# Letting the filter steps of a convolution lead TensorE a little in the source's order, in the last quarter of a two-layer encoder

## The chip, the cores and the metric

The kernel runs on one core of a Trainium2 chip. The metric is the time of one execution on the device in microseconds (us). TensorE (PE in the profile) multiplies matrices, VectorE (DVE) and ScalarE (ACT) work on rows of elements, GpSimd (POOL) adds and multiplies tiles, and SyncE (SP) issues the transfers between memory and the core.

## The reference

Two layers work on 2048 positions of 1024 channels. A layer normalizes its input, projects it to 28 groups of 128 channels, feeds four groups of heads, and projects their gated outputs back; a final normalization follows.

```python
def hybrid_layer(x, norm_g, w_in, w_out, ...):
    h = rmsnorm(x, norm_g)
    proj = jnp.einsum("bsd,de->bse", h, w_in)
    ...
    y_a = conformer_conv(a_u, a_v, ...) * jax.nn.silu(a_z)          # A: depthwise conv of width 31
    y_b = short_gated_conv(b_b, b_c, b_x, conv_b_w) * jax.nn.silu(b_z)   # B: width 3
    y_c = window_gqa(...) * jax.nn.silu(c_z)                        # C: attention in a window of 128
    y_d = neighborhood_attn(...) * jax.nn.silu(d_z)                 # D: attention on a 2-D grid
    y = jnp.concatenate([y_a, y_b, y_c, y_d], axis=-1)
    return x + jnp.einsum("bse,ed->bsd", y, w_out)

def conformer_conv(u, v, conv_w, conv_b, ln_g, ln_b):
    h = u * jax.nn.sigmoid(v)
    h = depthwise_conv(h, conv_w) + conv_b      # 31 taps
    h = layernorm(h, ln_g, ln_b)                # over the 256 channels of A
    return jax.nn.silu(h)
```

## The kernel before

Positions are cut into four chunks of 512 (0 to 3). Channels lie on partitions. Every float32 product is made of three matmuls on two rounded parts of each operand (`s0h`, `s0l` or `s1h`, `s1l` for the activations, `whi`, `wlo` for the weights), so one 128-channel tile of output for one chunk, called a job here, takes 24 matmuls `mm` of 128x512.

The work stands in eight blocks of jobs: layer 0's input projection for chunks 0 and 1 and then for 2 and 3, layer 0's output for chunks 0 and 1, and so on. The last three blocks are those of this case: layer 1's input projection for chunks 2 and 3 (28 weight tiles for two chunks, 56 jobs, "the input block"), layer 1's output for chunks 0 and 1 (16 jobs, "the first output block") and for chunks 2 and 3 (16 jobs, "the last output block").

Between the matmuls runs everything else, as Python generators that `point()` advances once per 8 matmuls:

- Attention units (`unit`, 64 in a layer): one unit treats 128 queries of two heads: scores `s`, softmax on VectorE and ScalarE, four to eight transposes `pt`, the weighted sum `o`, then `ou`, `oy` and `ag` on VectorE; after every fourth unit `ag` is stored to `Y`. Units start in a fixed order (D and C of chunk 0, D and C of chunk 1, and so on), and in the last stage every second point may start one.
- Filter steps ("taps", `tap_steps`): convolution A of a chunk and a half of its channels is 31 passes of VectorE over `accA`. `point()` emits taps while VectorE's counted time `clk["dve"]` lies behind TensorE's counted time `clk["pe"]` plus `LEAD`, which is 0. Both counters are sums of costs written into the program: every VectorE instruction adds to the one, every matmul to the other.
- Norms (`ln_steps`, `conv_ln`): when both halves of a chunk have their 31 taps, the LayerNorm of A follows: a sum on GpSimd (`lns`), a matmul with ones (`lnm`), squares, a second sum, `lnv` on TensorE, thirteen small VectorE steps for the root, `rb` on TensorE, then scale, tanh and gate (`ga` is loaded from `G`), and `accA` is stored to `Y`. Chunk 3 has a second, 15 columns wide norm for the last positions.
- A chunk's output jobs need its `Y` loaded and split (`place_y_steps`, into `s0l` or `s1l`). Chunk c's `Y` of convolution A is complete only when chunk c+1's norm is done too, since a chunk's filter is stored 15 positions late.

A scheduler then moves the instructions of each engine about, by priorities that follow the source's order, and within buffers that are handed out in the source's order: five temporaries `t`, two PSUM tiles for `s`, `lnm`, `lnv`, `rb` and `cs` together, four `accA`. So a step that stands late in the source can get its buffers only after those before it.

The first job of every odd chunk in layer 1's output waits in the source until no taps are left (`idle_until(lambda: not taps)` in `out_jobs`): it advances points and adds 1.8 to `clk["pe"]` each time.

Of the kernel before, what the change touches and what calls it, by code (L numbers as in the profile page):

```python
# [58 lines left out]
RU, RD = 3, 3  # L59
PF, UNITS, SPACING = 7, 4, 5  # L60
PF_LATE, UNITS_LATE, SPACING_LATE = 3, 6, 2
LEAD = 0.0
KSB, VTB, WB = 3, 3, 3

E_A_U, E_A_V, E_A_Z = 0, 2, 4
# [6 lines left out]
def trunk(ctx, tc, xT, w_in, w_out, par, sink, rpb, fg, trig, cmask, dmask, out):  # L72
    nc = tc.nc
    pe, act, dve, pool, sp = nc.tensor, nc.scalar, nc.vector, nc.gpsimd, nc.sync
# [37 lines left out]
    clk = {"pe": 0.0, "dve": 0.0}  # L112
# [19 lines left out]
    dve = Counted(dve)  # L132
# [37 lines left out]
    evs, bg, units, taps = [], [], [], deque()  # L170
    waiting, done = [], set()
    current, gap, points, begun, turn = [None], [0], [0], [0], [0, 0]
    pace = {"spacing": SPACING, "units": UNITS, "pf": PF}

    def advance(lst):
        for g in list(lst):
            if next(g, "end") == "end":
                lst.remove(g)

    def point():  # L180
        advance(evs)
        advance(units)
        gap[0] += 1
        points[0] += 1
        if waiting and gap[0] >= pace["spacing"] and len(units) < pace["units"] and begun[0] < turn[0] + QSB:
            group = current[0] or next((w for w in waiting if w[0]()), None)
            if group:
                current[0] = group
                gap[0] = 0
                g = group[1].popleft()()  # L190
                if not group[1]:
                    waiting.remove(group)
                    current[0] = None
                units.append(g)
                next(g)
        advance(bg)
        while taps and clk["dve"] < clk["pe"] + LEAD:
            tap()

    def tap():  # L200
        if next(taps[0], "end") == "end":
            taps.popleft()

    def idle_until(cond):
        n = 0
        while not cond():
            point()
            clk["pe"] += 1.8
            n += 1
            assert n < 4000, "nothing more happens"  # L210
# [648 lines left out]
    def run(j):  # L859
# [18 lines left out]
        for i, (k_, pt, hf, wi, k, rhs) in enumerate(seq):  # L878
            mm(pt, jb["ws"][hf][wi][:, k, :], rhs, n[k_] == 0, n[k_] == 3 * KT - 1, 0.228)
            n[k_] += 1  # L880
            if i % GRP == GRP - 1:
                g = i // GRP
                point()
                if g in work:
                    work[g]()
                for k2, p2 in zip(jb["keys"], pts):
                    if n.get(k2) == 3 * KT:
                        n[k2] = -1
                        evs.append(jb["ev"](k2[-1], p2))
# [6 lines left out]
    def in_jobs(l, half):  # L896
# [31 lines left out]
        def mark(i):  # L928
            ks = marks[i] if isinstance(marks[i], list) else [marks[i]]

            def late():
                yield from hold(8)
                for k in ks:
                    done.add(k)
            bg.append(late())
# [93 lines left out]
    then(o10[1], y_place(1, 3, 1))  # L1029

    def late():
        pace.update(spacing=SPACING_LATE, units=UNITS_LATE, pf=PF_LATE)
        return
        yield

    then(i10[1], late)

    for l in range(DEPTH):
# [138 lines left out]
```

## Time and profile before

| what | us |
|---|---|
| three runs | 2089.10, 2096.69, 2099.12 |
| median | 2096.69 |
| the profiled execution | 2092.12 |
| its span in the trace | 2090.3 |
| TensorE matmuls busy | 1967.2 (94%) |
| TensorE weight loads busy | 1638.5 (78%) |
| VectorE busy | 1553.1 (74%) |
| ScalarE busy | 1040.1 (50%) |

The profiled execution's own time is 1.8 us longer than its span. In the trace, times count from the start of the span; a line such as L135 is that of a helper through which all matmuls go, so instructions are told apart by the names of their tiles. Instructions of one group may overlap at their ends, so a sum of durations can exceed the busy time.

### The profile page before, as it was taken

How to read it: one execution, taken by the hardware profiler on the slowest of the kernel's cores; microseconds unless marked ns; L12 is line 12 of the kernel's file. 1: busy time of each engine (PE TensorE's matmuls, PEld its weight loads, DVE VectorE, ACT ScalarE, POOL GpSimd, SP SyncE). 2: the span in 40 equal slices, each digit the busy share in tenths (PEclk: the TensorE clock that was granted, in tenths of full speed). 3: DMA queues.
4: the chain of work that ended last, by engine and by line, in shares of the span. 5: the costliest groups of instructions: out<-in, count | busy, mean ns of one | idle time of the engine just before them, and what ended most of it. 6: DMA issues, size and time to landing. Idle time of an engine off the chain costs nothing.

```text
span 2090.3 us, 29475 instructions
## 1 busy us (share of the span) xinstructions
PE 1967.2 (94%) x9436; PEld 1638.5 (78%) x9436; DVE 1553.1 (74%) x3531; ACT 1040.1 (50%) x2217; POOL 181.6 (9%) x158
## 2 busy tenths in 40 slices
PE   5899999999999999899999999989999899996697
PEld 4778888787888878788888888878888788885585
DVE  6734799968985677776659998755995567866855
ACT  4435434523355466566654446532237566665542
POOL 0610000071010000000100000001000000100100
PEclk9999999999999999999999999999999999998698
DMA  9985533576455479867653467863638866577353
GB/s 281 305 280 175 150 121 92 170 257 200 151 172 171 158 246 305 242 201 236 183 164 119 143 179 220 244 197 105 179 132 252 227 193 207 154 221 221 120 177 115
DMA packets 233850, 400.65 MB, mean 192 GB/s; under 512 B 26848, under 2 KB 92000, under 8 KB 233440
## 3 DMA queue, kind: packets, MB, share of 16 engines
q1 hardware_dynamic: 233696, 398.77, 62.2%
q8 instruction: 75, 1.23, 0.3%
q14 instruction: 79, 0.65, 0.1%
HBM read 297.68 MB, written 105.61 MB: 193 GB/s over the span
## 4 chain that ended last, share of the span: by engine, by line
PE 71%; DMA 14%; DVE 9%; ACT 2%; issue 2%; SPq 1%; POOL 1%; DVEq 0%; POOLq 0%; ACTq 0%
PE mm L135 59%; PE o L135 3%; PE s L135 3%; PE pt L716 3%; DMA prob<-bias 2%; DMA wraw<-in_w_in_dram 2%; DVE wlo L128 1%; DMA s1l<-Y 1%; DVE xt L128 1%; DMA qs<-QD 1%; DMA qs<-QC 1%; DMA wraw<-in_w_out_dram 1%; POOL bmo L786 1%; DMA Y<-accA 1%; DVE accA L128 1%
## 5 line engine op out<-in xcount | busy, mean ns | idle before, releaser
L135 PE MATMUL mm<-s1h,whi 128*128 128x512 f32 x1152 | 458.8, 399 | 22.5 <-ACT s1h L218 10.8
L218 ACT CAST whi<-wraw 128x512 fp32r<-128x512 f32 x400 | 246.6, 618 | 444.9 <-PE mm L135 348.9
L135 PE MATMUL mm<-s1l,whi 128*128 128x512 f32 x1152 | 457.8, 398 | 6.2 <-DVE s1l L128 6.2
L135 PE MATMUL mm<-s0h,whi 128*128 128x512 f32 x1152 | 455.4, 396 | 7.0 <-ACT s0h L218 5.3
L135 PE MATMUL mm<-s0l,whi 128*128 128x512 f32 x1152 | 454.4, 395 | 4.9 <-DVE s0l L128 4.9
L135 PE MATMUL mm<-s1h,wlo 128*128 128x512 f32 x1152 | 455.2, 397 | 4.0 <-DVE wlo L128 4.0
L135 PE MATMUL mm<-s0h,wlo 128*128 128x512 f32 x1152 | 455.3, 396 | 1.0 <-DVE wlo L128 0.7
L128 DVE TENSOR_TENSOR wlo<-wraw,whi 128x512 fp32r<-128x512 f32 x400 | 289.3, 725 | 159.7 <-ACT whi L218 142.4
L128 DVE SCALAR_TENSOR_TENSOR accA<-gA,par,accA 128x512 f32<-128x512 f32 (+1 forms) x480 | 352.8, 774 | 0.6
L135 PEld LDWEIGHTS mm<-s1h,whi 128*128 128x128 f32 x1152 | 219.6, 191 | 69.8 <-ACT s1h L218 12.1
L135 PEld LDWEIGHTS mm<-s1l,whi 128*128 128x128 f32 x1152 | 219.9, 191 | 51.0 <-DVE s1l L128 7.5
L135 PEld LDWEIGHTS mm<-s0h,whi 128*128 128x128 f32 x1152 | 218.2, 190 | 51.5 <-ACT s0h L218 5.7
L135 PEld LDWEIGHTS mm<-s1h,wlo 128*128 128x128 f32 x1152 | 219.7, 191 | 49.4 <-DVE wlo L128 5.9
L135 PEld LDWEIGHTS mm<-s0l,whi 128*128 128x128 f32 x1152 | 218.2, 189 | 50.2 <-DVE s0l L128 6.3
L135 PEld LDWEIGHTS mm<-s0h,wlo 128*128 128x128 f32 x1152 | 218.2, 189 | 45.5 <-DVE wlo L128 3.2
L689 ACT ACTIVATE prob<-prob,mn 128x384 f32<-128x384 f32 (+4 forms) x256 | 155.3, 607 | 116.1 <-DVE mn L128 115.0
L706 ACT ACTIVATE prob<-prob,sm 128x384 f32<-128x384 f32 (+4 forms) x256 | 142.2, 602 | 49.8 <-DVE sm L128 43.9
L128 DVE TENSOR_TENSOR pth<-pt,pth 128x512 fp32r<-128x512 f32 (+3 forms) x248 | 138.5, 573 | 32.6 <-ACT pth L218 31.6
L135 PE MATMUL s<-ks,qs 128*128 128x384 f32 (+4 forms) x512 | 129.6, 357 | 21.1 <-DMA qs<-QC 7.0
L218 ACT CAST pth<-pt 128x512 fp32r<-128x512 f32 (+3 forms) x248 | 115.0, 495 | 66.6 <-PE pt L716 46.1
L135 PE MATMUL o<-pth,vt 128*128 128x256 f32 (+2 forms) x784 | 129.6, 297 | 8.2 <-DVE oy L128 5.2
L135 PEld LDWEIGHTS o<-pth,vt 128*128 128x128 f32 (+2 forms) x784 | 117.4, 199 | 20.7 <-issue 4.1
(120 smaller groups left out, 2039.5 us busy)
## 6 DMA issues: line engine op xcount, KB each, us to landing
wraw<-in_w_in_dram SPq DMA_DIRECT2D x272, 256.0 KB
wraw<-in_w_out_dram SPq DMA_DIRECT2D x128, 256.0 KB
qs<-QD SPq DMA_DIRECT2D x128, 128.0 KB
qs<-QC SPq DMA_DIRECT2D x128, 128.0 KB
G<-g SPq DMA_DIRECT2D x48, 256.0 KB
vt<-VD SPq DMA_DIRECT2D x144, 72.0 KB
xt<-in_xT_dram SPq DMA_DIRECT2D x20, 512.0 KB
KD<-t SPq DMA_DIRECT2D x32, 256.0 KB
```

The source lines that it names most:

```text
L128: return fn(*a, **kw)
L135: pe.matmul(out=out, lhsT=lhsT, rhs=rhs, start=start, stop=stop)
L218: act.copy(out=hi, in_=src)
L689: act.activation(out=t[:, hh, :n], in_=t[:, hh, :n], func=AF.Exp, bias=mn[:, hh:hh + 1], scale=-1.0, accum_out=sm[:, hh:hh + 1])
L706: act.activation(out=t[:, hh, :n], in_=t[:, hh, :n], func=AF.Copy, scale=sm[:, hh:hh + 1])
L716: pe.transpose(out=tp[:kw, b_, hh, :], in_=t[:, hh, kb * kw:(kb + 1) * kw], identity=ident)
L786: pool.tensor_tensor(out=t[:, hh, :sz].rearrange("p (g r c) -> p g r c", r=rr, c=C), in0=mkv, in1=Ms[2 * p + hh][:, r0:r0 + R, c0:c0 + C]. ...
```

## The change

Layer 1's last stage gets a lead of its own. `pace` holds the lead, `point()` reads it there, and `late()`, which already sets the units' pace behind layer 1's first input projection, sets it to 6.0. Nothing is computed otherwise.

```diff
-LEAD = 0.0
+LEAD, LEAD_LATE = 0.0, 6.0
...
-    pace = {"spacing": SPACING, "units": UNITS, "pf": PF}
+    pace = {"spacing": SPACING, "units": UNITS, "pf": PF, "lead": LEAD}
...
         advance(bg)
-        while taps and clk["dve"] < clk["pe"] + LEAD:
+        while taps and clk["dve"] < clk["pe"] + pace["lead"]:
             tap()
...
     def late():
-        pace.update(spacing=SPACING_LATE, units=UNITS_LATE, pf=PF_LATE)
+        pace.update(spacing=SPACING_LATE, units=UNITS_LATE, pf=PF_LATE, lead=LEAD_LATE)
```

The engines' orders agree, but for the numbers in names, up to the input block's third job. There the norm of chunk 0 (of layer 1) now stands; before it stood three jobs, 72 matmuls, later. Three places further on follow.

The first is TensorE's order around the 512 wide norm of chunk 3 (`lnm`). Before, among transposes `pt` and sums `o` of the last units:

```order
L135 MATMUL s_19296<-ks_19078,qs_19241 128x256 x2
L135 MATMUL s_19299<-ks_19078,qs_19241 128x256 x2
L716 MATMUL pt_19208<-ident,prob_19109 128x128 x4
L716 MATMUL pt_19245<-ident,prob_19155 128x128 x4
L135 MATMUL lnm_19470<-lns_19446,ones 128x512
```

And now, within the input block (`mm_15640` is chunk 2's job of weight tile 17, `mm_15641` chunk 3's):

```order
L135 MATMUL mm_15640<-s0l_13660,whi_15491 128x512
L135 MATMUL mm_15640<-s0h_13656,wlo_15492 128x512
L135 MATMUL lnm_15638<-lns_15567,ones 128x512
L135 MATMUL mm_15640<-s0h_13657,whi_15595 128x512
L135 MATMUL mm_15640<-s0l_13661,whi_15595 128x512
L135 MATMUL mm_15640<-s0h_13657,wlo_15596 128x512
L135 MATMUL mm_15641<-s1h_14037,whi_15491 128x512
```

The norm of chunk 3 has moved from behind the first output block, where the scores of all 64 units are already made, into the input block, 37 jobs earlier. Chunk 2's norm moves from the first output block's third job to the input block's weight tile 13, and the 15 columns wide one to weight tile 21.

The second place is TensorE's order behind the last matmul of the first output block (`mm_19789`). Before:

```order
L135 MATMUL mm_19789<-s1h_18403,wlo_19784 128x512
L135 MATMUL cs_18940<-ones,acc_18144 128x1 x4
L135 MATMUL s_18968<-ks_18779,qs_18893 128x384 x2
L716 MATMUL pt_18846<-ident,prob_18558 128x128 x4
L716 MATMUL pt_18851<-ident,prob_18558 128x128 x2
L135 MATMUL o_18803<-pth_18737,vt_18597 128x256 x2
L135 MATMUL o_18803<-pth_18740,vt_18597 128x256
```

Now the same steps of chunk 0's final norm (`cs`) and of a unit stand between matmuls of the last output block's second job (`mm_19951`):

```order
L135 MATMUL mm_19951<-s0l_19135,whi_19904 128x512
L135 MATMUL cs_19096<-ones,acc_18289 128x1 x4
L135 MATMUL s_19124<-ks_18904,qs_19018 128x384 x2
L135 MATMUL mm_19951<-s0h_19131,wlo_19905 128x512
L135 MATMUL mm_19951<-s0h_19131,whi_19904 128x512
L135 MATMUL mm_19951<-s0l_19135,whi_19904 128x512
L135 MATMUL mm_19951<-s0h_19131,wlo_19905 128x512
L135 MATMUL mm_19951<-s0h_19132,whi_19945 128x512
L716 MATMUL pt_18971<-ident,prob_18691 128x128 x4
```

Before, from that last matmul on, no `mm` stands in TensorE's order until all units are done. Now chunk 2's eight output jobs and the first halves of three of chunk 3's (228 matmuls) stand ahead of the last unit's `o`.

The third place is the end of the units on TensorE. Now (`mm_20308`, `mm_20360`, `mm_20424` are chunk 3's first three jobs):

```order
L135 MATMUL cs_20343<-ones,acc_19993 128x1 x4
L135 MATMUL o_19899<-pth_19863,vt_19320 128x256 x4
L135 MATMUL rb_20397<-ident,rc_83 128x128 x4
L135 MATMUL mm_20308<-s1h_20030,whi_20302 128x512
L135 MATMUL mm_20360<-s1h_20030,whi_20354 128x512
L135 MATMUL mm_20424<-s1h_20030,whi_20418 128x512
L135 MATMUL mm_20308<-s1l_20034,whi_20302 128x512
```

Before, the last unit's `o` stands ahead of the last output block's first matmul:

```order
L135 MATMUL o_19401<-pth_19389,vt_19080 128x256 x4
L135 MATMUL rb_19868<-ident,rc_83 128x128 x4
L135 MATMUL rb_19895<-ident,rl_19873 128x15
L135 MATMUL mm_19981<-s0h_19937,whi_19799 128x512
L135 MATMUL mm_20018<-s0h_19937,whi_19990 128x512
```

The rows of `s1h_20030` are the second halves of chunk 3's jobs, which read the attention's part of `Y`; 156 matmuls are left from there.

## Rows read from the trace of the kernel before

**Rows 1.** the page: busy us (share of the span) and instructions

```profile
PE 1967.2 (94%) x9436; PEld 1638.5 (78%) x9436; DVE 1553.1 (74%) x3531; ACT 1040.1 (50%) x2217; POOL 181.6 (9%) x158
```

**Rows 2.** stretches: start:end length, PE, PEld, DVE, ACT, POOL busy, clock, DMA, GB/s

```profile
1569.90:1762.70 192.80, 186.15 (x951) 156.58 (x951) 123.83 (x341) 124.59 (x281) 10.30 (x8) 0.99 0.75 221
1762.70:1826.00 63.30, 63.22 (x335) 53.24 (x333) 51.82 (x143) 44.09 (x102) 7.68 (x5) 1.00 0.53 161
1826.00:1834.80 8.80, 5.76 (x27) 4.37 (x26) 8.03 (x27) 7.05 (x21) 0.00 (x0) 0.78 0.89 268
1834.80:1899.00 64.20, 62.02 (x314) 51.80 (x313) 41.47 (x112) 38.62 (x91) 0.00 (x0) 0.98 0.74 207
1899.00:1976.00 77.00, 46.39 (x214) 38.46 (x213) 57.34 (x204) 43.50 (x111) 4.54 (x5) 0.68 0.49 145
1976.00:2026.30 50.30, 48.31 (x193) 38.91 (x194) 33.90 (x56) 23.18 (x43) 3.85 (x2) 0.92 0.71 225
2026.30:2072.10 45.80, 45.77 (x209) 37.53 (x207) 26.41 (x50) 14.13 (x23) 0.00 (x0) 1.00 0.32 108
2072.10:2090.30 18.20, 3.10 (x17) 2.75 (x16) 8.90 (x23) 1.21 (x2) 0.00 (x0) 0.63 0.31 116
```

**Rows 3.** the chain, start us, us, what: matmuls back to back

```profile
1509.11 55.34 PE mm L135 x244
```

**Rows 4.** the chain: an earlier norm among matmuls

```profile
1421.04 0.86 PE lnm L135 x2
1430.98 0.79 PE lnv L135 x8
1440.32 0.89 PE rb L135 x8
```

**Rows 5.** VectorE in order of time: first and last filter steps of this stage

```profile
1448.72 0.54 DVE L128 TENSOR_SCALAR accA<-gA,par 128x512 f32<-128x512 f32 x1
...
1566.65 0.76 DVE L128 SCALAR_TENSOR_TENSOR accA<-gA,par,accA 128x527 f32<-128x527 f32 x1
```

**Rows 6.** GpSimd in order of time: the sum of chunk 3's norm

```profile
1823.38 1.76 POOL L493 TENSOR_TENSOR lns<-accA,accA 128x512 f32<-128x512 f32 x1
```

**Rows 7.** TensorE in order of time: the norm of chunk 3

```profile
1941.91 1.90 PE L135 MATMUL lnm<-lns,ones 128*128 128x512 f32 x2
...
1949.52 1.87 PE L135 MATMUL lnv<-ones,lns 128*128 128x1 f32 x8 [0.52 <-POOL lns L507]
...
1958.44 1.91 PE L135 MATMUL rb<-ident,rl 128*128 128x128 f32 x8
```

**Rows 8.** SyncE's queue: chunk 3's norm stored, chunk 2's Y loaded

```profile
1964.80 3.64 SPq L539 DMA_DIRECT2D Y<-accA  x2
1970.62 0.56 SPq L332 DMA_DIRECT2D s0l<-Y  x1
```

**Rows 9.** TensorE: the last mm of one block, the first of the next

```profile
1898.57 0.39 PE L135 MATMUL mm<-s1h,wlo 128*128 128x512 f32 x1
...
1975.97 1.22 PE L135 MATMUL mm<-s0h,whi 128*128 128x512 f32 x2 [1.99 <-ACT s0h L218]
1976.99 0.63 PE L135 MATMUL mm<-s0l,whi 128*128 128x512 f32 x1
1977.41 0.63 PE L135 MATMUL mm<-s0h,wlo 128*128 128x512 f32 x1
```

**Rows 10.** the chain: stores to Y and loads from it

```profile
1632.06 3.63 DMA Y<-ag
...
1824.43 4.61 DMA Y<-accA
...
1829.65 5.84 DMA s1l<-Y
...
1998.09 8.91 DMA s1l<-Y
```

**Rows 11.** VectorE from 1899 to 1976 by lines: the units' last step

```profile
L128 DVE SCALAR_TENSOR_TENSOR ag<-oy,ag 128x128 f32<-128x128 f32 x13 | 3.7, 285 | 0.1
```

## The prediction

> **What bounds the kernel now.** I read the page first, then the busy time cut by stage at the ends of the last blocks, then the chain, then single engines in order of time where the stages showed a hole.
>
> The page has TensorE busy for 94% of the span [rows 1], which suggests that there is nothing to win. The stages say otherwise [rows 2]: from 1762.7 to 1826 TensorE is busy for 63.22 of 63.30 us, but from 1899 to 1976 for 46.39 of 77, at a granted clock of 0.68. The last matmul of the first output block is issued at 1898.57, the first of the last output block at 1975.97 [rows 9]: for 77 us no projection runs, while 13 units finish [rows 11].
>
> What was waited for? Chunk 2's `Y` is loaded at 1970.62, right after chunk 3's norm has been stored from 1964.80 [rows 8], and that norm's three TensorE steps stand at 1941.91, 1949.52 and 1958.44 [rows 7]. Its input was there long before: the last filter step ended at 1567.4 [rows 5] and GpSimd had the sum at 1825 [rows 6]. So the norm waits for its place in the order and for buffers, not for data. The second hole is smaller: 1826 to 1834.8, where chunk 2's norm is stored and loaded for chunk 1's outputs [rows 10].
>
> **What moves.** The number of instructions stays. The order of each engine shows all norms of layer 1's last stage within the input block. So the outputs of chunks 1 and 2 need no late norm any more; what is late next is the last unit, for chunk 3's second half.
>
> *The input block gets longer.* One norm in the matmul stream costs TensorE 0.86 + 0.79 + 0.89 = 2.5 us [rows 4]; two wide ones and a narrow one move in: 6 us. VectorE, ScalarE and GpSimd have room for their part (123.83, 124.59 and 10.30 of 192.80 us [rows 2]). The norms' six loads and six stores now go through SyncE's queue among the loads of bias and queries there; each stands behind its own GpSimd step, and what is queued behind it are loads for units two ahead. I cost that at nothing, covered by that lead; uncovered it is one landing, 3.63 to 4.61 us [rows 10], per norm.
>
> A new wait: TensorE's order now has chunk 2's `lnm` at weight tile 13, 169 matmuls into a stretch of 244 that took 55.34 us, 0.2268 each [rows 3]: at 1509.1 + 169 × 0.2268 = 1547.4. In the trace the last filter step ended 20 us later. But the filter steps of this stage began at 1448.72, 8.4 us after `rb` of chunk 0's norm at 1440.32 [rows 4, 5], because a norm must release `accA`; that norm now stands 72 matmuls earlier, 72 × 0.2268 = 16.3 us. So the last step should come at 1567.4 − 16.3 = 1551. With GpSimd's sum behind it TensorE waits 3 to 6 us, at worst 20, at best nothing. I take 3, since the same earlier start also helps VectorE in a stretch where it had idle time.
>
> *The first output block* took 1762.7 to 1898.9. TensorE's work in it is 63.2 us to 1826, 5.76 × 0.78 = 4.5 us at full clock in the hole, and 62.02 behind it: 129.7. One norm goes (2.5), some 1 us was lower clock: 126 us.
>
> *The tail to the last unit.* Ahead of the last unit's `o` stand now 228 matmuls: 51.7 us. A unit's share of TensorE: the input block's last stretch was busy for 186.15 us, held 576 matmuls (130.6) and about 26 units, so 55.5 / 26 = 2.1 us. About 14 units are open when the first output block ends: 29.4. With `cs` and `rb` of two final norms (3.6) that is 85 us of TensorE. VectorE: the two stretches from 1899 to 2026.3 held 57.34 + 33.90 = 91 us [rows 2], without the norms (thirteen small and six wide steps twice, about 10) 81. Two engines near their limit do not overlap perfectly: at VectorE's shares of 82% (1762.7 to 1826) and 91% (the hole) 81 us take 99 or 89. The bounds are 85 (TensorE alone) and 99; I take 91.
>
> A rule speaks for more. In the Trainium skill, Perfetto Trace Analysis (Identifying the Most-Contended Engine) says that matmul busy time overstates how near TensorE is to its limit, and that the weight loads' busy share is the better measure. Here that share is 53.24 of 63.30, 84%, in the densest stretch, so by the rule 85 us could shrink to 71, and VectorE's 89 would decide: 2 us less. The trace has 244 matmuls start 0.2268 us apart with nothing waited for, so I keep 85.
>
> *From the last unit to the end.* Its `ou`, `oy` and `ag` (1.5 us), the store of `Y` (3.63), the load (5.84, or 8.91 when output stores share the engines as they do in this tail) and the first split (1.3): 12 to 15 us, and 14 taken [rows 10]. This wait is new; before, chunk 3's loads hid behind chunk 2's outputs. Then 156 matmuls, 35.4 us, and 2 us for the clock, which fell to 0.68 where units ran alone. The end from 2072.1 to 2090.3 stays: 18.2.
>
> **The sum**: 1762.7 + 6 + 3 + 126 + 91 + 14 + 35.4 + 2 + 18.2 = 2058.3, and 1.8 outside the span gives 2060. The profiled execution took 2092.1, so the change saves 32 us against it, and 37 against the median of 2096.7. With the low ends (no wait, norms in TensorE's idle 6.6 us of the input block, 85, 12) it is 2043; with the high ones (20, 99, 15, two landings) 2094, which all at once is unlikely; two thirds of the way, 2082.
>
> **Rivals.**
>
> *The units set the pace.* In the first output block 15 units took 136.1 us, 9.1 each; 14 at that pace need 127 us rather than 91 and the time is 2096, no change. For it: the units are a long chain over three engines and the transfers, and at 1899 to 1976 they took 5.9 each with TensorE half empty. Against it: in the first output block TensorE was full, with 25.6 matmuls for each unit; the tail has 16.3.
>
> *The moved norms stall the input block* (the other side). All engines run in order, so TensorE waits at `lnm`, `lnv` and `rb` when the step between is late, with the whole projection behind it. Where nothing useful stood between, the hops took 7.6 and 8.9 us [rows 7]: three norms uncovered are 50 us, in place of the 3 taken 2107, slower. It turns the result above 40 us. For it: VectorE is full while the filter steps run, and the wait at weight tile 13 rests on a shift that I estimate. Against it: 37 and 41 matmuls stand between chunk 2's three steps now, 8.4 and 9.3 us of cover.
>
> *The clock.* From 1976.99 to 1977.41 two matmuls start 0.42 us apart, against 0.2268 at full clock. If TensorE stayed at 1.2 GHz through the new tail, its 228 matmuls would take 44 us more: 2104. For it: the clock was 0.68 with units alone, and 0.92 in the stretch behind. Against it: 1.00 from 1762.7 to 1826, where units and matmuls alternate as they now do in the tail. The Trainium skill, TensorE: Matmul & The Clock Gate (HAM oscillation), says that a matmul stream broken by waits falls back to the low clock each time; the row of 1899 to 1976 agrees with it, the row of 1762.7 to 1826 shows no such break.
>
> **Chances.** The forecast's mechanism 0.83 (its own range 2043 to 2082), the units' pace 0.08 (no change), the stalls 0.05 (0.03 of it slower), the clock 0.02 (half of it slower), other 0.02 (slower). About 0.5%, 10 us, is what a measurement of this kernel can tell from no change. Faster, below 2086: 0.83; within: 0.11; slower, above 2107: 0.06. The range for 8 in 10 is 2040 to 2088: it reaches just to where the units' pace would hold back most of the gain.
>
> **What would show it.** Right: no stretch of more than 20 us without `mm` between 1760 and the last unit; `lnm` of chunk 3 near 1590; the wait at 1826 gone; a hole of 12 to 15 us just ahead of chunk 3's second halves, released by a load of `Y`; a last `ag` near 1990. Wrong: waits on `lnm`, `lnv` or `rb` in the input block of more than 10 us in all, or waits of TensorE for `pth`, `mn` or `qs` in the tail, so that the last `ag` comes after 2010.

## The result, and the profile after

The changed kernel takes 2069.52 us (median of 4 runs, 2065.16 to 2072.73) against 2095.42 for the kernel before beside it (4 runs): a ratio of 0.9878, interval 0.9845 to 0.9911. So 26 us are saved; 32 to 37 were forecast. The profiled execution took 2071.99 us, with a span of 2070.2.

The page's first line is as little help as before: TensorE's share is the same 94%, 16.7 us less of it [rows 1].

```profile
PE 1950.5 (94%) x9436; PEld 1627.5 (79%) x9436; DVE 1546.9 (75%) x3531; ACT 1038.6 (50%) x2217; POOL 179.7 (9%) x158
```

Where the time went shows in the stages. These stretches answer to [rows 2] (columns as there): the input block's second half; the first output block; the last output block up to the last unit in four pieces; from the last unit to chunk 3's second halves; the matmuls left; the end.

```profile
1577.50:1775.20 197.70, 190.89 (x991) 161.62 (x990) 138.50 (x395) 135.70 (x308) 18.29 (x17) 0.99 0.77 223
1775.20:1902.50 127.30, 122.73 (x622) 101.89 (x621) 88.83 (x240) 80.37 (x191) 1.66 (x1) 0.99 0.67 200
1902.50:1927.60 25.10, 25.04 (x137) 20.86 (x135) 20.94 (x67) 19.19 (x46) 0.00 (x0) 1.00 0.73 201
1927.60:1941.00 13.40, 5.67 (x22) 4.26 (x20) 11.31 (x29) 8.52 (x23) 0.00 (x0) 0.60 0.95 301
1941.00:1990.00 49.00, 48.97 (x256) 41.88 (x257) 37.02 (x108) 27.68 (x66) 0.00 (x0) 0.97 0.43 132
1990.00:2007.10 17.10, 6.87 (x33) 5.70 (x31) 15.42 (x40) 5.02 (x11) 0.00 (x0) 0.65 0.75 253
2007.10:2015.00 7.90, 2.10 (x9) 1.80 (x9) 5.01 (x11) 1.28 (x3) 0.00 (x0) 0.50 0.61 189
2015.00:2052.70 37.70, 37.70 (x156) 30.35 (x156) 18.43 (x29) 12.02 (x20) 0.00 (x0) 0.95 0.27 93
2052.70:2070.20 17.50, 3.12 (x17) 2.75 (x16) 8.90 (x23) 1.22 (x2) 0.00 (x0) 0.61 0.32 120
1902.50:2007.10 104.60, 86.55 (x443) 72.70 (x441) 84.69 (x241) 60.40 (x142) 0.00 (x0) 0.88 0.62 190
```

The 77 us without projection [rows 9] are gone: the last output block starts where the first ends. The last row is "the tail" of all that follows, from there to the last unit's `ag`: 104.6 us.

Chunk 3's norm stands where the order put it. TensorE in order of time (start, duration, instruction): no wait is noted at it, where before it came 346 us later [rows 7].

```profile
1595.17 0.40 PE L135 MATMUL mm<-s0h,wlo 128*128 128x512 f32 x1
1595.40 1.02 PE L135 MATMUL lnm<-lns,ones 128*128 128x512 f32 x2
1595.86 0.80 PE L135 MATMUL mm<-s0h,whi 128*128 128x512 f32 x1
```

What TensorE waited for in the input block, by what ended the wait (total us, times, longest): of the norms only one `lnv`, 0.9 us.

```profile
PE s L135 <- DMA vt<-VD: 3.6, 1, 3.6
PE mm L135 <- DVE s1l L128: 3.5, 1, 3.5
...
PE lnv L135 <- POOL lns L507: 0.9, 1, 0.9
```

The filter steps start at 1430.96 (1448.72 before) and end at 1550.95, ahead of chunk 2's `lnm` at 1552.79 [rows 5]. VectorE in order of time:

```profile
1430.96 1.15 DVE L128 TENSOR_SCALAR accA<-gA,par 128x512 f32<-128x512 f32 x1 [0.25 <-DMA Y<-accA]
...
1550.19 0.76 DVE L128 SCALAR_TENSOR_TENSOR accA<-gA,par,accA 128x527 f32<-128x527 f32 x1
```

The tail has two bad stretches that were not forecast. The first is the one of 13.4 us above. TensorE in it, with what ended each wait:

```profile
1932.78 1.51 PE L716 MATMUL pt<-ident,prob 128*96 128x128 f32 x6 [4.07 <-DVE pth L128]
...
1935.82 1.62 PE L135 MATMUL o<-pth,vt 128*128 128x256 f32 x6 [1.06 <-DMA out_dram<-xf]
1937.24 1.48 PE L135 MATMUL s<-ks,qs 128*128 128x384 f32 x4
1941.03 0.80 PE L135 MATMUL mm<-s0h,whi 128*128 128x512 f32 x1 [2.30 <-DVE xf L128]
1941.62 0.63 PE L135 MATMUL mm<-s0l,whi 128*128 128x512 f32 x1
1942.05 0.63 PE L135 MATMUL mm<-s0h,wlo 128*128 128x512 f32 x1
```

The chain over the same stretch (the work that ended last, followed back; start, us, what) says why: chunk 0's eight final scalings (`xf` at 1925 to 1932) stand on VectorE ahead of `pth`, then a load of chunk 2's residual, which needs a buffer that chunk 0's results leave, then its first eviction (the addition that empties a PSUM tile) at 1940.29, which frees a tile for `mm`.

```profile
1927.54 1.32 DVE xf L128 x2
1928.87 0.59 issue
1929.45 1.41 DVE xf L128 x2
1930.86 0.60 DVE acc L128
1931.46 0.66 DVE xf L128
1932.12 0.93 DVE pth L128 x2
...
1934.25 3.98 DMA xf<-X
1938.24 2.05 issue
1940.29 0.70 DVE xf L128
1941.03 7.17 PE mm L135 x24
```

The second is at the end. The 228 matmuls that stand ahead of the last unit are done by 1990; the units run 17 us longer, with VectorE busy for 15.42 of them. It ends with the last `ag` and what follows it on the chain:

```profile
2006.90 0.20 DVE ag L128
2007.10 0.03 DVE rn L128
2007.13 1.99 DMA Y<-ag
...
2009.14 5.15 DMA s1l<-Y
...
2014.31 0.63 ACT s1h L218
```

### The profile page after: what moved, and what is told of

Its sections match the earlier page's. It is cut to its first block, busy times and chain, and to the rows that moved or that the text cites. A ratio compares the mean times of both kernels' runs of the same rounds, so it can differ in the third digit from the quotient of the medians.

```text
span 2070.2 us, 29461 instructions
## 1 busy us (share of the span) xinstructions
PE 1950.5 (94%) x9436; PEld 1627.5 (79%) x9436; DVE 1546.9 (75%) x3531; ACT 1038.6 (50%) x2217; POOL 179.7 (9%) x158
## 4 chain that ended last, share of the span: by engine, by line
PE 69%; DMA 13%; DVE 10%; issue 4%; ACT 2%; POOL 1%; SPq 1%; DVEq 0%; ACTq 0%; POOLq 0%
PE mm L135 58%; PE o L135 3%; PE s L135 3%; PE pt L716 3%; DMA wraw<-in_w_in_dram 3%; DMA s1l<-Y 2%; DVE wlo L128 1%; DMA prob<-bias 1%; DMA X<-xo 1%; DMA wraw<-in_w_out_dram 1%; DVE accA L128 1%; DVE xf L128 1%; DMA G<-g 1%; POOL bmo L786 1%; DVE s0l L128 1%
## 5 line engine op out<-in xcount | busy, mean ns | idle before, releaser
L716 PE MATMUL pt<-ident,prob 128*128 128x128 f32 (+2 forms) x784 | 116.5, 276 | 10.8 <-DVE pth L128 10.8
```

The source lines that it names most:

```text
L716: pe.transpose(out=tp[:kw, b_, hh, :], in_=t[:, hh, kb * kw:(kb + 1) * kw], identity=ident)
```

## The experiments

The times are medians of all runs, each ratio is against the kernel before on the same chip; the columns behind them are read from one profiled execution each. `e1` to `e4` shared one chip, `e5` to `e8` another, `e9` to `e12` a third. The last column is the time from the input block's first matmul to the end. It leaves out the code ahead of that block, which is the same in all and scatters.

| run | us | ratio (interval) | tail us | TensorE busy | VectorE busy | from the input block |
|---|---|---|---|---|---|---|
| before | 2095.42 | | | | | 711.1 |
| the change | 2069.52 | 0.9878 (0.9845, 0.9911) | 104.6 | 86.55 | 84.69 | 685.8 |
| e1_norm3_late | 2100.09 | 1.0015 (1.0003, 1.0027) | | | | 717.1 |
| e2_flush_no_lead | 2082.42 | 0.9927 (0.9912, 0.9943) | 107.6 | 88.45 | 88.39 | 697.3 |
| e3_no_final_scale | 2064.02 | 0.9838 (0.9823, 0.9853) | 96.9 | 86.13 | 73.77 | 680.0 |
| e4_lead_1p5 | 2066.80 | 0.9848 (0.9820, 0.9875) | 110.4 | 89.80 | 88.74 | 685.9 |
| e5_change_again | 2070.30 | 0.9885 (0.9860, 0.9910) | 107.7 | 88.23 | 84.86 | 689.4 |
| e6_cs_in_mm | 2066.84 | 0.9862 (0.9839, 0.9884) | 103.3 | 87.86 | 81.05 | 686.4 |
| e7_residual_t2 | 2067.59 | 0.9864 (0.9833, 0.9896) | 98.1 | 83.53 | 83.81 | 683.9 |
| e8_both | 2066.34 | 0.9851 (0.9821, 0.9880) | 96.6 | 83.55 | 79.55 | 680.0 |
| e9_acc_pool | 2058.22 | 0.9838 (0.9817, 0.9858) | 97.7 | 82.96 | 82.90 | 680.3 |
| e10_all_three | 2055.73 | 0.9808 (0.9788, 0.9829) | 91.5 | 80.82 | 75.36 | 676.5 |
| e11_scale_off_dve | 2052.31 | 0.9795 (0.9778, 0.9811) | 87.4 | 77.69 | 73.50 | 669.2 |
| e12_three_no_lead | 2087.83 | 0.9959 (0.9942, 0.9976) | | | | 704.9 |

### Is it the place of chunk 3's norm?

```diff
     def ln_steps(l, c):
         while ("az", l, c) not in done:
             yield
+        while (l, c) == (1, 3) and ("c", 1, 3, 1, 3) not in done:
+            yield
```

The lead stays, but chunk 3's norm waits in the source until the last unit is done.

> The change with one part undone: chunk 3's norm is held in the source until the last unit is done; lead 6, chunk 2's norm early as in the change. Theory (the gain is the place of chunk 3's norm: only it lets the last output block run beside the last units): the last mm of the first output block and the first of the last one are 75 us or more apart again, and the time is 2088 to 2110, no gain left. Rival (the gain comes from the filter steps' earlier start and the missing hole at 1826): 2068 to 2080, with the 77 us hole of no weight.

The whole gain is gone. The hole between the output blocks is back, though chunk 2's norm still comes early, at 1549.0. It is 95.6 us long where it was 77, since the first output block ends earlier (1892.7, not 1899) and this norm is held until the last unit. Its stretch, and chunk 3's `lnm` and the first `mm` of the last output block:

```profile
1892.70:1988.30 95.60, 53.02 (x237) 44.46 (x236) 70.40 (x235) 49.94 (x127) 6.78 (x8) 0.65 0.58 179
```

```profile
1952.74 1.06 PE L135 MATMUL lnm<-lns,ones 128*128 128x512 f32 x1
...
1988.35 1.22 PE L135 MATMUL mm<-s0h,whi 128*128 128x512 f32 x2 [6.94 <-ACT s0h L218]
```

### Does the norm's place do without the lead?

```diff
-LEAD, LEAD_LATE = 0.0, 6.0
+LEAD, LEAD_LATE = 0.0, 0.0
...
         if jb["pre"]:
             jb["pre"]()
+        while j == FLUSH[0] and taps:
+            tap()
```

With lead 0, all taps that are left are emitted ahead of the input block's weight tile 13 (`FLUSH[0]` is that job's number).

> Lead 0 everywhere, but whatever filter steps are left are emitted at once at weight tile 13 of the input block, so that the norms of chunks 2 and 3 follow there. Theory (only the place of the norms counts, not that the filter leads TensorE): as the change, 2064 to 2076. Rival (the lead itself, 6 us at every point, does the work): 2085 to 2097.

The time, 2082.42, fell between the two expectations. The late hole is gone as with the lead (chunk 3's `lnm` at 1567.0). But chunk 0's norm is not earlier (1422.4, against 1402.7), so filter steps run from 1450 to 1565 with VectorE full, and TensorE waits for VectorE's evictions behind them. First the stretch, then TensorE in it:

```profile
1540.00:1571.00 31.00, 24.86 (x96) 18.83 (x95) 30.07 (x43) 10.24 (x18) 6.90 (x5) 0.92 0.28 85
```

```profile
1558.30 0.50 PE L135 MATMUL mm<-s1h,whi 128*128 128x512 f32 x1 [3.20 <-DVE rhl L128]
...
1570.62 0.77 PE L135 MATMUL mm<-s0h,whi 128*128 128x512 f32 x1 [2.50 <-DVE rhl L128]
```

The input block's first half takes 205.3 us there and 193.1 with the lead: 12 us, of which the second half gives 3 back. So the input block can stall, as a rival had it, at a quarter of that rival's size, but by another wait: in that half TensorE waits 5.7 us for evictions (`rhl`) and 0.4 us for `lnm`. The lead is spared it, it seems, because chunk 0's norm moves up by 72 matmuls as well; nothing was run in which that norm alone moves.

### Is the lead's size of account?

```diff
-LEAD, LEAD_LATE = 0.0, 6.0
+LEAD, LEAD_LATE = 0.0, 1.5
```

> The change with a lead of 1.5 us instead of 6. Theory (it is a threshold: any small lead lets the last filter steps be emitted before the units crowd them out): 2062 to 2078, as the change. Rival (the gain grows with the lead): a quarter of 26 us, 2086 to 2094.

A quarter of the lead gives the same: 2066.80, an interval that overlaps the change's, with chunk 3's `lnm` at 1601.9. So the lead acts as a switch, somewhere between 0 and 1.5: it decides whether the last filter steps are emitted before the units or after all of them. The tail is longer here (110.4 us), with 15 units left for it where the change has 14.

### Why the tail is 104.6 us and not 91

```diff
                 for k in range(KT):
                     xk = xos[(l, c, k)]
-                    dve.scalar_tensor_tensor(out=xk, in0=xk, scalar=fg_t[:, k:k + 1], in1=rs, ...)
+                    if c > 1:
+                        dve.scalar_tensor_tensor(out=xk, in0=xk, scalar=fg_t[:, k:k + 1], in1=rs, ...)
```

The final scaling of chunks 0 and 1 is left out, so the output is not the reference's.

> The change, with the final norm's scaling by VectorE left out for chunks 0 and 1 (their output is stored unscaled): 16 passes of 0.69 us fewer, and their tiles come free without waiting for it. Theory (the tail took 104.6 us instead of 91 because chunk 0's and chunk 1's scaling and storing stand in front of the units' steps and of the tiles that chunk 2's residual needs): the hole of 13.4 us at 1927.6 and the wait of 4.9 at 1996 go, 2052 to 2060. Rival (the units' own chain sets the pace of the tail): 2066 to 2072.

2064.02, between the two expectations. The hole of 13.4 us and the wait of 4.9 are gone, and the tail is 96.9 us, so the scalings account for some 8 of the 13.6 us that the forecast lacked. What the rest is, the next four runs asked, the first of them being the change once more.

> The changed kernel itself once more, beside the next three on one chip. Both theories: within 5 us of its 2069.5, and in the trace again a tail (end of the first output block to the last unit's sum) of 103 to 107 us with a hole of 12 to 15 us without matmuls some 25 us after the last output block's start, and a second half-empty stretch of about 17 us ahead of the last unit's end.

It repeats: 2070.30, a tail of 107.7, so two traces of one kernel differ by 3 us there. The next edit is to the norm that issues the scalings. Chunk 0's last matmul ends at 1836.1 and its last sum of squares at 1843.06, but its `cs` runs at 1912.30, 69 us later (the 76 expected below count from the matmul), since `cs` and `rb` share two PSUM tiles (tag `s`) with the units' scores, which are handed out in the source's order.

```diff
-        pt = T(ps, [P, CH], F32, "s", 2, "cs")
+        pt = T(ps, [P, CH], F32, *(("mm", 3) if l == DEPTH else ("s", 2)), "cs")
...
-        rb = T(ps, [P, CH], F32, "s", 2, "rb")
+        rb = T(ps, [P, CH], F32, *(("mm", 3) if own else ("s", 2)), "rb")     # own: the final norm
```

> The change, and the PSUM tiles of layer 1's last norm (cs, rb) come from the pool of the output blocks (mm, 3 tiles) instead of the scores' pool (s, 2 tiles), which is handed out in the order of the source and lags behind with the units. Theory (the tail is 13.6 us longer than forecast because chunk 0's final norm runs 76 us after its data are ready, in the middle of the last output block, where its eight scalings and its stores stand ahead of the units' and the residual's work): cs of chunk 0 runs within 20 us of chunk 0's last eviction, inside the first output block, the 13 us hole goes, the tail is 90 to 96 us and the time 2055 to 2062. Rival (the units' own chain sets the length of the tail, whatever stands between): the tail stays at 102 to 106 and the time within 4 us of the changed kernel's, 2066 to 2073; the holes only move.

`cs` of chunk 0 now runs at 1841.4, and no stretch like that of 13.4 us is left; still the tail is 103.3 us and the time 2066.84. My theory in this form fell: chunk 2's outputs end 8.5 us sooner (67.9 us into the tail, not 76.4), and the units take the 35 us behind them instead of 28. The holes moved, as the rival said, and from the input block on the kernel takes 686.4 us, as the change does (685.8 and 689.4).

```diff
-  held["xx"] = T(gp, [P, 2, CH], F32, "xt", XTB, "xf")
+  held["xx"] = T(gp, [P, 2, CH], F32, *(("t2", TH) if c == 2 and dt < 4 else ("xt", XTB)), "xf")
```

> The change, and the first two pairs of chunk 2's residual tiles (xf<-X) are put into the t2 buffers instead of the xt buffers, which chunk 0's stores free only after its final scaling. Theory: of the 13.4 us hole the part after VectorE is done with the scalings (xf loads issued at 1934.25, matmuls again at 1941.03) goes, some 6 us: tail 97 to 100, time 2062 to 2066; the scalings themselves (6.5 us of VectorE ahead of pth) still hold the units. Rival (the hole is VectorE's alone, the load is hidden): no change, 2066 to 2073, the hole as long as before, its last matmul wait on pth.

The tail was as the theory had it: 98.1 us, the hole gone, and VectorE's work in it is that of the change (83.81 us). The whole tail, and its first 60.3 us:

```profile
1912.30:2010.40 98.10, 83.53 (x442) 69.82 (x440) 83.81 (x241) 60.42 (x143) 0.00 (x0) 0.94 0.63 195
1912.30:1972.60 60.30, 59.02 (x305) 49.17 (x304) 51.59 (x142) 40.16 (x98) 0.00 (x0) 1.00 0.74 220
```

The median was not: 2067.59, with runs from 2055.78 to 2075.56, cannot be told from the change on that chip.

`e8_both` joins the last two edits.

> The two edits before together. Theory: as with the norm's tiles in the output blocks' pool alone (2055 to 2062), since once chunk 0's norm and stores come early its xt buffers are free when chunk 2's residual wants them: within 2 us of that run. Rival (two separate costs that add): 4 to 6 us below that run.

2066.34, like each edit alone. In none of these three does the median separate from the change's. The traces say more: with the hole gone by `e7` or `e8` the tail is 6.5 to 11 us shorter than in the two traces of the change, with `e6` it is not, and from the input block on only `e8` (680.0) lies clear of the change's two. So what the hole is worth stays open, from nothing to some 10 us, and hangs on how it is removed. The next edits take work from VectorE in place of moving it.

```diff
-            dve.tensor_tensor(out=acc, in0=acc, in1=sq, op=ALU.add)
+            (pool if l == DEPTH - 1 and c < 2 else dve).tensor_tensor(out=acc, in0=acc, in1=sq, op=ALU.add)
```

> The change, and the running sums of squares of the output blocks of chunks 0 and 1 (acc<-acc,sq, 14 of 0.68 us in all on VectorE, most of them in the tail) go to GpSimd, which is idle there. Nothing leaves the computation, no buffer is added. Theory (VectorE's queue sets the tail: 84.7 us busy of 104.6, and the units stand in it behind scalings and sums): the units finish sooner, the tail is 93 to 99 us, time 2058 to 2064. Rival 1 (the units' chain over three engines sets the tail, VectorE has room): the tail stays at 103 to 107, time 2066 to 2072. Rival 2 (GpSimd's sum, 1.2 to 1.5 us where VectorE takes 0.68, makes evictions late): slower, 2072 to 2080.

2058.22 and a tail of 97.7 lie where the theory had them, but not for its reason. The interval overlaps the change's first one, and from the input block on it is `e8`'s time (680.3). VectorE's busy time in the tail hardly fell (82.90), though seven sums (0.68 us each) and one unit are gone from it: while GpSimd worked on seven sums of chunk 1, chunk 0's eight scalings took 11.00 us where `e7` has 5.37, and TensorE stood idle behind them for 9.1 us.

```profile
1911.06 11.02 POOL L823 TENSOR_TENSOR acc<-acc,sq 128x512 f32<-128x512 f32 x7 [80.25 <-ACT sq L822]
1912.95 11.00 DVE L128 SCALAR_TENSOR_TENSOR xf<-xf,fg_t,rs 128x512 f32<-128x512 f32 x8
1925.15 1.44 PE L135 MATMUL s<-ks,qs 128*128 128x256 f32 x4 [9.12 <-DVE mn L128]
```

```profile
1936.88 5.37 DVE L128 SCALAR_TENSOR_TENSOR xf<-xf,fg_t,rs 128x512 f32<-128x512 f32 x8
```

(The first three lines are of `e9`, the last of `e7`.) What shortens this tail is that 16 units were finished in the first output block where the change finished 15, and 13 were left; so it is in `e10` and `e11`. The order has units some matmuls earlier there, and VectorE had fewer sums; no run separates the two.

`e10_all_three` joins this edit to `e8_both`.

> The change with all three edits: the last norm's PSUM tiles from the output blocks' pool, chunk 2's residual in the t2 buffers, the sums of squares of chunks 0 and 1 on GpSimd. Theory (each shortens what TensorE waits for in the tail, and none is hidden behind another): tail 88 to 94, time 2052 to 2060. Rival (after the hole is gone the last units' chain sets the end, which no edit touches): tail 96 to 99 as with the first two, time 2064 to 2068.

`e11_scale_off_dve` also takes the scalings from VectorE:

```diff
+                    if c < 2:
+                        act.activation(out=xk, in_=xk, func=AF.Copy, scale=fg_t[:, k:k + 1])
+                        pool.tensor_tensor(out=xk, in0=xk, in1=rs, op=ALU.mult)
+                    else:
-                    dve.scalar_tensor_tensor(out=xk, in0=xk, scalar=fg_t[:, k:k + 1], in1=rs, ...)
+                        dve.scalar_tensor_tensor(out=xk, in0=xk, scalar=fg_t[:, k:k + 1], in1=rs, ...)
```

> As the run before, and the final scaling of chunks 0 and 1 is taken from VectorE too: ScalarE multiplies by the weight, GpSimd by the row's factor (16 scalings that held VectorE 11.1 us of the tail). Theory: VectorE falls to about 65 us of the tail and no longer sets it; TensorE's 84 us do: tail 86 to 92, time 2050 to 2058. Rival (ScalarE, 60 us busy there, gets 10 us more ahead of the units' casts): no better than the run before, or up to 5 us slower.

Both times and tails came out within their theory: 2055.73 and 2052.31. VectorE did not, with 73.50 us in `e11` where about 65 were expected; the last section says why. The tails, of `e9`, `e10` and `e11` in this order (one line of the stretches of each):

```profile
1892.00:1989.70 97.70, 82.96 (x434) 70.22 (x433) 82.90 (x226) 56.51 (x133) 10.55 (x7) 0.92 0.64 199
```

```profile
1904.20:1995.70 91.50, 80.82 (x433) 67.95 (x430) 75.36 (x215) 53.81 (x129) 1.30 (x1) 0.95 0.63 194
```

```profile
1899.70:1987.10 87.40, 77.69 (x419) 65.57 (x417) 73.50 (x199) 52.59 (x124) 13.53 (x9) 0.97 0.60 196
```

The granted clock rises with each as holes go, and TensorE's idle time in the tail falls from 18.05 us (104.6 less 86.55) to 14.7, 10.7 and 9.7. `e11` computes all that the reference asks for. It is 17 us below the change by the ratios, and not told apart from `e10`.

`e12_three_no_lead` has the edits of `e10` and lead 0.

> The three edits with the lead put back to zero, that is, on the kernel before. Theory (the change's gain is the place of chunk 3's norm, the edits act in a tail that only the change makes): chunk 3's norm again near 1950, a hole of over 60 us between the output blocks, within 10 us of the kernel before (2084 to 2096), so the lead is worth 26 us or more beside the edits too. Rival (the edits and the lead gain on the same idle time): the edits alone give most of it, 2065 to 2080.

It takes 2087.83. Chunk 3's norm is late again and the hole between the output blocks is 62.2 us:

```profile
1934.67 1.10 PE L135 MATMUL lnm<-lns,ones 128*128 128x512 f32 x2 [0.24 <-DVE mn L128]
```

So the lead is worth 2087.83 − 2055.73 = 32 us beside the edits (28 by the table's last column), no less than the 26 alone, and the edits without it 7 us.

## Why the prediction was right, and what it had wrong

The mechanism was right: the norm of chunk 3 had waited for its place, not for data. With its place alone the gain goes (`e1`), and the norms put early without the lead bring 14.6 us of it (`e2`), net of the stall in the input block. Term by term, by the profiled execution, which ended 12 us after the forecast:

- *The unchanged part.* The input block began at 1384.4, at 1379.2 in the profile before. The code ahead of it is the same, so 5.2 us are scatter.
- *The input block*: 7.3 us longer (193.1 and 197.7 us for its halves, 190.7 and 192.8 before), 9 forecast. The wait at weight tile 13 was cost at 3 us and is nothing in the trace: the filter steps began 17.8 us sooner where I had worked out 16.3 (22.9 when both are counted from the block's start), and the last ended at 1550.95. That this is the forecast's 1551 is luck: the block began 5.2 us late, and counted from its start the steps began 6.6 us sooner than worked out.
- *The first output block*: 127.3 us, 126 forecast. The wait at 1826 is gone.
- *The tail to the last unit*: 104.6 us, 91 taken. **This is the term that was mis-sized**, and it lies outside its bounds (85 to 99). Both loads were near: TensorE 86.55 us, forecast 85; VectorE 84.69, forecast 81. The first is partly luck: at the clocks of its four pieces (1.00, 0.60, 0.97 and 0.65) the busy time comes to some 80 us of full clock, an estimate. What failed is how the two overlap. I had two shares of VectorE, 82% and 91%, the second from a stretch of 8.8 us, and took 91 us, near what the second gave; the tail ran at 81%, the share of the stretch in which matmuls and units alternate. The wait on `pth`, half of the sign of being wrong, came too, 8.9 us in all, with the last `ag` at 2007.1 and not near 1990. The runs say in part what sets the length. Order counts: with VectorE's work as it was, the tail without the hole was 98.1 us (`e7`), yet in `e6` the wait only moved to the end. VectorE's work counts: without the scalings it was 96.9 (`e3`). And in `e9` to `e11` one unit fewer was left for it; there it went down to 87.4 with VectorE at 73.50 us and TensorE at 77.69. How much of the 13.6 us each of these makes, no run settles.
- *From the last `ag` to chunk 3's second halves*: 7.9 us, 14 taken, below the range of 12 to 15. The store took 1.99 and the load 5.15 us, where [rows 10] had 3.63 and 5.84 to 8.91; and I had counted 1.5 us of `ou`, `oy` and `ag` that lie ahead of the last `ag`'s end.
- *The rest*: 37.7 us for the matmuls left (37.4) and 17.5 for the end (18.2).

With the differences 5.2 − 1.7 + 1.3 + 13.6 − 6.1 + 0.3 − 0.7 the 12 us close.

Of the rivals, the units' pace was the nearest to the truth: not 127 us, but 14 units at 7.5 us each, and at the end TensorE has no projection left while they finish. The stall in the input block did not occur with the lead; `e2` shows one of 12 us, by evictions and not by the norms' steps. The clock fell to 0.60 in the hole, and behind it matmuls start 0.43 us apart, at 1.2 GHz, from 1941.62 to 1943.76; over the tail it is 0.88, by the estimate above some 6 us of the 44 priced. By the rule on weight loads that I weighed (the Trainium skill, Perfetto Trace Analysis, Identifying the Most-Contended Engine) VectorE decides and the tail is 89 us. That page of the Trainium skill calls matmul busy time no good measure of headroom and names the weight loads' share as one to use instead; that busy time overstates is how I read it. The trace does not agree with the 89 us: the tail took 104.6, and from 1941 to 1990 TensorE was busy for 48.97 of 49.00 us with the weight loads at 41.88, 85%; so a share like the 84% of before stands here beside a TensorE that never stood idle.

## What to carry to other kernels

When an instruction runs long after its data are ready, ask what stands before it in the order that hands out its buffers; a small number in a planner can act as a switch there, so try a smaller value before tuning it. When two engines are both near full in a stretch, take their overlap from a stretch with the same mixture and not from one in which one of them runs alone. A hole in the trace need not be worth its length: one edit that took it away left the stage as long, because the wait moved to its end, and another shortened it. So measure the whole stage behind an edit, from a point ahead of which nothing changed. When work is moved to an idle engine, look at how long the other engines' instructions take beside it.

## What was not expected of the hardware

The same instructions ahead of the input block ended between 1372.8 us (`e9`) and 1389.4 us (`e7`, on another chip) in the profiled executions: 16.6 us of scatter in code that no edit touches, as wide as most effects studied here. One kernel, the change, has 1384.4 and 1378.4. Differences of stages within one trace were of more use than single times.

VectorE and GpSimd were not independent. In `e9`, shown above, six scalings that ran beside GpSimd's sums took 1.31 to 1.77 us each; the two behind them, when GpSimd was done, took 0.74, as everywhere in the changed kernel's tail. GpSimd's sums went from 1.29 to 1.6 us. While GpSimd multiplied eight 128x512 tiles in `e11`, VectorE instructions on two columns took many times their usual length. GpSimd first, then VectorE in order of time:

```profile
1924.68 12.12 POOL L840 TENSOR_TENSOR xf<-xf,rs 128x512 f32<-128x512 f32 x8 [14.23 <-ACT rs L834]
```

```profile
1926.46 1.24 DVE L128 TENSOR_TENSOR sm<-sm,es 128x2 f32<-128x2 f32 x1
...
1931.20 0.83 DVE L128 TENSOR_TENSOR es<-mn,sink 128x2 f32<-128x2 f32 x1
...
1935.59 1.37 DVE L128 SCALAR_TENSOR_TENSOR ag<-oy,ag 128x128 f32<-128x128 f32 x1
```

In the changed kernel none of the 128 such instructions on two columns (`es`, `sm`) took over 0.163 us; here four did, three of them in this stretch, in which GpSimd's multiplies took 1.3 to 1.8 us each. Instructions that read one operand from PSUM kept their length (`xf<-xf,mm` 0.67, `ou<-o,ou` 0.40). The Trainium skill, SBUF — State Buffer (Who interferes with whom), says that VectorE and GpSimd share one pair of ports under an exclusive lock, and that a VectorE instruction with two inputs in SBUF contends for it with a GpSimd instruction that reads SBUF. The traces agree with it; no run here tells it from another cause. It cost VectorE some 4.8 us in this stretch of `e11`, nearly as much as the eight scalings that were taken from its tail (5.4 us), and 6.7 us in `e9`, more than the seven sums (4.8 us). In `e10` only one sum fell into the tail, and no VectorE instruction took longer.
